# A gated product transposed by VectorE and two queues instead of TensorE, and two top-k rounds moved later

## The chip, the cores and the metric

The kernel runs on one core of a Trainium2 chip. The metric is the device time of one launch in microseconds (us); lower is better. The core has five engines with a queue each: TensorE (PE, with its weight loads shown as PEld), VectorE (DVE), ScalarE (ACT), GpSimd (POOL) and SyncE (SP, which only issues transfers).

## The reference

One decoder block over 512 tokens of width 1024, in float32. Two token mixers run beside each other; their gated sum is projected and added to the input, and a squared-ReLU MLP follows.

```
h = rmsnorm(x); proj = h @ w_in         # u, v_g, q, k, v, q_idx, k_idx, w_idx, gates
# branch a: spatial gating, in 4 chunks c of 128 tokens and 4 groups g of 128 channels
v_g = layernorm(gelu(v_g))
s   = einsum('gts,bcsgd->bctgd', tril(w_s), v_g) + b_s
y_a = gelu(u) * s                        # the "gated product", 512 x 512
# branch b: attention over the 128 keys with the highest index score (top-k)
score = sum_h w_idx * relu(q_idx @ k_idx^T), causal;  sel = top_k(score, 128)
y_b = softmax(rope(q) @ rope(k)[sel]^T / 8) @ v[sel]
merged = sig(g0) * (y_a @ w_out_a) + sig(g1) * (y_b @ w_out_b)
x = x + merged @ w_o
x = x + relu(rmsnorm(x) @ w_ff_in)^2 @ w_ff_out
return rmsnorm(x)
```

## The kernel before

Every float32 product is made of three TensorE passes on split operands: each operand is written as a high part in a matmul format and a low part that holds the remainder (`split`, line 50: ACT copies the high part, DVE or POOL subtracts to get the low part). Weights come in tiles of 128 x 1024 numbers in a fixed sequence: `w_load` issues the transfer (on ACT's queue for the first 24, on SP's after that), `w_conv` splits it (the subtraction of tile 24 and later is DVE's, "wl"), and using tile n calls for the conversion of tiles n+1 and n+2. The buffers are two raw tiles and three of each part.

The program is one list. Products are generators (`gemm`): one step is three matmuls. `fill(n)` lets the next n steps of the queued generators run at that place of the program, so that TensorE has work while VectorE does something else. Evacuations are called one step after the last product (`later`, `tick`). A planner then orders each engine's instructions: it plays the program with modelled costs, takes among the ready instructions the one that stands first in the program, and gives tile slots from the pools as they come free. `keep_in_program_order` pins an instruction behind the one that was written just before it for its engine. Transposed products and evacuations use two pools of four PSUM tiles each, "ps" (gates, keys, queries, the products oa) and "pa" (spatial products, transposes, scores).

The stretch around the change, in the order of the program:

- Lines 535 to 542: 16 rounds of top-k on the index scores `sc[1..3]` (384 query rows in three tiles). In a round, MAX8 finds the eight largest of each row and MATCH_REPLACE marks them as taken. Each round is followed by `fill(5)`; the layer norm of v_g is woven into some. Lines 543 and 544 turn the marks into a mask that is added to the attention scores.
- Line 569: the keys' projection (first four heads) starts; its rotation (`rope`, lines 342 to 356) runs on DVE once both halves are there: four products with cosR and sinR (L347, L348), two sums (L349), and the splits (L351, L352). `k_done` then copies the parts by 32 transfers on POOL's queue into the layout of the scores.
- Lines 574 to 580: the spatial products sg, 12 matmuls of 512 columns, read as four runs of 128; DVE makes the gated product in place in `u` (L579): tokens lie on partitions.
- Lines 583 to 590: the queries' projection is queued. The products `y_a @ w_out_a` need the channels on partitions, so TensorE transposes `u` in 16 blocks of 128 x 128 into PSUM (L588, "yt"), four at a time behind each step of the queries; ACT copies the high part yaTh (L589), DVE subtracts for the low part yaTl (L590).
- Lines 594 to 619: gate gb (first tile), then the products oa of branch a (`branch_a`, eight tiles of 12 matmuls) follow, each evacuated by DVE (L611). The heads of the attention begin behind six of the oa tiles.

At the end of the kernel, `ff_last` makes the last output tile in two column halves (L942 adds a half, L1011 sums its squares, L1015 multiplies it by the gain), POOL raises the mean square to the power -1/2 (L1014), and `store` scales and stores the rows.

Of the kernel before, what the change touches and what calls it, by code (L numbers as in the profile page):

```python
# [12 lines left out]
AF = mybir.ActivationFunctionType  # L13
ALU = mybir.AluOpType

P = 128
# [17 lines left out]
def hybrid_block_kernel(ctx: ExitStack, tc: tile.TileContext, A: dict, out: bass.AP):  # L34
# [9 lines left out]
    def bank(name, tag="ps"):  # L44
        return ps.tile([P, 512], F32, tag=tag, bufs=4, name=name)

    def f32(ap):
        return ap.bitcast(F32)
# [10 lines left out]
    def half(tag, bufs, name):  # L59
        pool, dt = (G, F32) if tag == "yb" else (E, FR)  # L60
        return pool.tile([P, 4, S], dt, tag=tag, bufs=bufs, name=name)
# [26 lines left out]
    def fill(n):  # L88
        while n > 0 and todo:
            try:  # L90
                next(todo[0])
                n -= 1
                tick()
            except StopIteration:
                todo.pop(0)
# [436 lines left out]
            yield  # L532

    ln = layer_norm()
    for n in range(TOPK // 8):
        for i in range(NT - 1, 0, -1):
            DVE.max(out=m8[i], in_=sc[i])
        for i in range(NT - 1, 0, -1):
            DVE.match_replace(out=sc[i], in_to_replace=m8[i], in_values=sc[i], imm_value=TAKEN)
        if n >= 4:  # L540
            next(ln, None)
        fill(5)
    for i in range(1, NT):
        DVE.tensor_scalar(sc[i], sc[i], TAKEN, -BIG, op0=ALU.is_gt, op1=ALU.mult)
    while todo:
        fill(8)

# [21 lines left out]
    fill(12)  # L569
    u = dst_uv["u"]  # L570
    vgh, vgl = vghl
    yaT = [half("ybt", 2, f"yaT{c}") for c in "hl"]
    for g in range(4):
        b = bank(f"sg{g}", "pa")
        c = slice(g * P, (g + 1) * P)
        PE.matmul(b, wsh[:, g], vgl[:, :, c], start=True, stop=False)
        PE.matmul(b, wsl[:, g], vgh[:, :, c], start=False, stop=False)
        PE.matmul(b, wsh[:, g], vgh[:, :, c], start=False, stop=True)
        DVE.scalar_tensor_tensor(u[:, :, c], b.rearrange("p (c d) -> p c d", d=P), bs[:, g:g + 1],  # L579
                                 u[:, :, c], op0=ALU.add, op1=ALU.mult)  # L580
    fill(4)
    todo.append(rope_tiles(W_Q0, "q0", q_done))
    fill(11)
    for g in range(4):
        fill(1)
        b = bank(f"yt{g}", "pa")
        for c in range(NT):
            tc.keep_in_program_order(PE.transpose(b[:, c * P:(c + 1) * P], u[:, c, g * P:(g + 1) * P], ident))  # L588
        ACT.activation(yaT[0][:, g], b, AF.Copy)  # L589
        DVE.tensor_tensor(yaT[1][:, g], b, f32(yaT[0][:, g]), op=ALU.subtract)  # L590
    while todo:
        fill(8)

# [13 lines left out]
    def branch_a(m):  # L607
        b = bank(f"oa{m}")

        def evac():  # L610
            DVE.tensor_tensor(mA[m], b, mA[m], op=ALU.mult)  # L611
        yield from gemm(b, W_OA[m], [yaT[0][:, k] for k in range(4)], [yaT[1][:, k] for k in range(4)], evac)


    todo.append(gate_b(0))
# [350 lines left out]
    def ff_last(fs):  # L966
        def term(dst, w, j, q, k, cols, first, last):
            wh, wl = w[q]
            t = slice(j * P, (j + 1) * P)
            fh, fl = fs[2 * q + k]  # L970
            PE.matmul(dst, fl[:, t], wh[:, k, cols], start=first, stop=False)
            PE.matmul(dst, fh[:, t], wl[:, k, cols], start=False, stop=False)
            PE.matmul(dst, fh[:, t], wh[:, k, cols], start=False, stop=last)
            tick()

        for c in range(2):
            b = [bank(f"f2_{c}_{j}", "pa") for j in range(NT)]
            ws_ = W_F2[c]
            w = {}

            def part(j, q):
                if q not in w:
                    w[q] = w_get(ws_[q], S)
                for k in range(2):
                    term(b[j], w, j, q, k, slice(0, S), q == 0 and k == 0, q == 1 and k == 1)
                if j == 0:
                    w_ahead(ws_[q])
                if q == 1:
                    a = acc[j][:, c * S:(c + 1) * S]
                    add_to(a, b[j], j)  # L990
                    finish(j, c)

            for j, q in [(j, q) for j in range(NT) for q in range(2)] if c else \
                    [(j, q) for q in range(2) for j in range(NT)]:
                if (c, j) != (1, NT - 1):
                    part(j, q)


        j = NT - 1
        bh = [b[j][:, :SH], bank("f2_last", "ps")[:, :SH]]  # L1000
        s = fss[:, j]
        gated[j] = tmp(f"fo{j}")
        store(j - 1)
        for n in range(2):
            cols = slice(n * SH, (n + 1) * SH)
            for q in range(2):
                for k in range(2):
                    term(bh[n], w, j, q, k, cols, q == 0 and k == 0, q == 1 and k == 1)
            a = acc[j][:, S + n * SH:S + (n + 1) * SH]
            add_to(a, bh[n], j)  # L1010
            DVE.tensor_tensor_reduce(out=jk2[:, cols], in0=a, in1=a, op0=ALU.mult, op1=ALU.add, scale=1.0 / D,  # L1011
                                     scalar=s[:, 2 - n:3 - n], accum_out=s[:, 1 + 2 * n:2 + 2 * n])
            if n == 1:
                POOL.tensor_tensor(s[:, 3:4], s[:, 3:4], mhalf[:, :1], op=ALU.pow)  # L1014
            DVE.tensor_tensor(gated[j][:, cols], a, gF[1][:, cols], op=ALU.mult)  # L1015

    fss = G.tile([P, NT, 4], F32, name="fss")
    gated = {}
# [28 lines left out]
    def store(j):  # L1047
        s = fss[:, j, 3:4]
        a, b = acc[j][:, :S], gated[j]
        if j == NT - 2:  # L1050
            ACT.activation(a, a, AF.Copy, scale=s)
        else:
            DVE.tensor_scalar(a, a, s, None, op0=ALU.mult)
        ACT.activation(b, b, AF.Copy, scale=s)
        nc.sync.dma_start(out[j * P:(j + 1) * P, :S], a)
        (nc.scalar if j == NT - 1 else nc.sync).dma_start(out[j * P:(j + 1) * P, S:], b)

    raw_load(0)
    raw_load(1)
# [35 lines left out]
def _col_tiles(w, cols):  # L1095

    k = w.shape[0] // P
    t = w[:, cols].reshape(k, P, -1, P)
    return np.ascontiguousarray(t.transpose(2, 1, 0, 3)).reshape(-1, P, k * P)
# [11 lines left out]
def _layout(x, norm1_g, w_in, w_s, b_s, sgu_ln_g, sgu_ln_b, w_out_a, w_out_b, w_o,  # L1111
            norm2_g, w_ff_in, w_ff_out, norm_f_g):
    c = np.ascontiguousarray
    x = np.asarray(x)[0]
    w = np.asarray(w_in)[0]
    cos, sin = _tables()
    k = KD
    a = {}
    a["xT"] = c(x.T.reshape(k, P, S).transpose(1, 0, 2))
    a["xn"] = c(x.reshape(NT, P, D).transpose(1, 0, 2))  # L1120
    g1 = np.asarray(norm1_g)[0].reshape(k, P).T
    a["x0"] = c(np.concatenate([g1, np.zeros_like(g1), a["xT"][:, 0]], axis=1))

    rows = np.arange(D).reshape(4, KD, 32).transpose(1, 0, 2).reshape(-1)
    a["xr"] = c(x.T[rows].reshape(k, P, S).transpose(1, 0, 2))
    a["g2"] = c(np.asarray(norm2_g)[0][rows].reshape(k, P).T)
    a["gf"] = c(np.asarray(norm_f_g).reshape(1, D))
    a["wa"] = c(np.concatenate([w[:, 2048:2560], w[:, 3072:3144]], axis=1).reshape(k, P, 584).transpose(1, 0, 2))
    cols = _rope_cols(2560) + _rope_cols(1536) + _rope_cols(1024) + list(range(3144, 5192))
    a["wt"] = _col_tiles(w, cols)  # L1130
    a["wuv"] = c(w[:, :1024].reshape(4, 2, P, 2, S).transpose(3, 0, 2, 1, 4)).reshape(8, P, 2 * S)
    a["ws"] = c(np.asarray(w_s)[0].transpose(2, 0, 1))
    a["bs"] = c(np.asarray(b_s)[0].T)
    a["lng"] = c(np.asarray(sgu_ln_g).reshape(1, S))
    a["lnb"] = c(np.asarray(sgu_ln_b).reshape(1, S))

    def pairs(t):
        n, p, f = t.shape
        return c(t.reshape(n // 2, 2, p, f).transpose(0, 2, 1, 3)).reshape(n // 2, p, 2 * f)

    a["woa"] = pairs(_col_tiles(np.asarray(w_out_a)[0], slice(None)))
    a["wob"] = pairs(_col_tiles(np.asarray(w_out_b)[0], slice(None)))
    a["wo"] = _col_tiles(np.asarray(w_o)[0], rows)
    a["f1"] = _col_tiles(np.asarray(w_ff_in)[0][rows], slice(None))
    f2 = np.asarray(w_ff_out)[0].reshape(16, 2, P, 2, S)
    a["f2"] = c(f2[14:].transpose(0, 3, 2, 1, 4)).reshape(4, P, 2 * S)
    a["f2p"] = c(f2[:14].transpose(0, 2, 1, 3, 4)).reshape(14, P, 4 * S)
    a["cs"] = c(np.stack([np.tile(cos.T, (4, 1)), np.tile(sin.T, (4, 1))], axis=1))
    a["csn"] = c(np.stack([cos, sin]).reshape(2, NT, P, 32).transpose(2, 0, 1, 3))
    return a  # L1150
# [17 lines left out]
```

## Time and profile before

| | us |
|---|---|
| time, median of 3 runs (692.12 to 692.24) | 692.13 |
| the profiled execution's own time | 692.15 |
| its span | 690.4 |
| PE busy | 682.8 (99%) |
| DVE busy | 549.3 (80%) |
| ACT busy | 341.3 (49%) |
| POOL busy | 136.4 (20%) |

Times in the rows are microseconds from the start of the span. A row of the order of time has the start, the duration, the engine, the line, the operation, what is written and read, its shape, how many instructions were merged in the row (x4), and in brackets for how long the engine had been idle before and what ended that. Matmuls are pipelined: a matmul of 512 columns is shown with 0.39, and the next one starts about 0.23 after it. The granted TensorE clock was full (0.999) over the span.

### The profile page before, as it was taken

What the parts mean: (1) busy time and instruction counts of PE and PEld (TensorE: products, weight loads), DVE (VectorE), ACT (ScalarE), POOL (GpSimd) and SP (SyncE); (2) the same over time, 40 slices, a digit from 0 to 9 for tenths busy, and PEclk for the clock granted to TensorE, in tenths of its full rate; (3) what the DMA queues carried; (4) which work ended last, traced back from release to release, by engine and by line L of the source; (5) the groups of instructions that cost most, each with busy time, mean ns of one, the idle gap of its engine ahead of it and who ended that gap; (6) DMA issues with size and microseconds to landing.
All of it is one profiled execution on the core that took longest, in us unless ns stands there. A gap on an engine that the chain in (4) does not pass through costs nothing.

```text
span 690.4 us, 8970 instructions
## 1 busy us (share of the span) xinstructions
PE 682.8 (99%) x3207; PEld 574.2 (83%) x3207; DVE 549.3 (80%) x1013; ACT 341.3 (49%) x593; POOL 136.4 (20%) x178
## 2 busy tenths in 40 slices
PE   9999999999999999999999999999999999999996
PEld 8998888888888888888888888888888888888885
DVE  5584999999768978786658756978788797878996
ACT  6634644432345636573336765366562635546143
POOL 0044347862730850000027000000000000000001
PEclk9999999999999999999999999999999999999999
DMA  8736122332841651324358332232333224134023
GB/s 323 273 99 196 63 95 86 98 94 66 246 143 62 168 169 62 108 76 149 125 195 229 96 122 91 88 127 61 130 114 122 77 67 163 61 122 123 0 62 122
DMA packets 26844, 84.12 MB, mean 122 GB/s; under 512 B 5168, under 2 KB 6832, under 8 KB 24752
## 3 DMA queue, kind: packets, MB, share of 16 engines
q1 hardware_dynamic: 16944, 48.38, 22.0%
q10 hardware_dynamic: 5760, 26.78, 11.3%
q0 software_dynamic: 4096, 8.40, 4.7%
q8 instruction: 25, 0.41, 0.3%
q14 instruction: 19, 0.16, 0.1%
HBM read 71.48 MB, written 2.10 MB: 107 GB/s over the span
## 4 chain that ended last, share of the span: by engine, by line
PE 98%; DVE 0%; issue 0%; ACT 0%; POOLq 0%; POOL 0%
PE f L159 8%; PE f L160 8%; PE f L158 8%; PE pp L927 6%; PE pp L928 6%; PE pp L926 6%; PE va L298 4%; PE gb L160 2%; PE gb L158 2%; PE gb L159 2%; PE wo L160 2%; PE ga L159 2%; PE ga L158 2%; PE wo L159 2%; PE wo L158 2%; PE ga L160 2%
## 5 line engine op out<-in xcount | busy, mean ns | idle before, releaser
L51 ACT ACTIVATE wh<-wr 128x1024 fp32r<-128x1024 f32 x88 | 92.8, 1056 | 77.8 <-issue 16.6
L52 DVE TENSOR_TENSOR wl<-wr,wh 128x1024 fp32r<-128x1024 f32 x67 | 81.4, 1218 | 28.6 <-ACT wh L51 28.5
L158 PE MATMUL f<-h2h,wl 128*128 128x512 f32 x256 | 99.6, 389 | 0.0
L159 PE MATMUL f<-h2l,wh 128*128 128x512 f32 x256 | 99.6, 389 | 0.0
L160 PE MATMUL f<-h2h,wh 128*128 128x512 f32 x256 | 99.6, 389 | 0.0
L51 ACT ACTIVATE u<-w2r 128x512 fp32r<-128x512 f32 x98 | 59.0, 625 | 75.7 <-DVE w2r L857 28.1
L927 PE MATMUL pp<-u,fp 128*128 128x512 f32 x196 | 76.2, 389 | 0.0
L928 PE MATMUL pp<-u,fp 128*128 128x512 f32 x196 | 76.2, 389 | 0.0
L52 DVE TENSOR_TENSOR u<-w2r,u 128x512 fp32r<-128x512 f32 x98 | 64.1, 684 | 12.3 <-ACT u L51 12.3
L926 PE MATMUL pp<-u,fp 128*128 128x512 f32 x196 | 72.0, 389 | 0.0
L938 DVE TENSOR_TENSOR P<-pp,P 128x512 f32<-128x512 f32 x84 | 54.4, 683 | 16.6 <-PE pp L928 16.6
L52 POOL TENSOR_TENSOR wl<-wr,wh 128x1024 fp32r<-128x1024 f32 x21 | 52.6, 2504 | 47.9 <-ACT wh L51 46.1
L1023 POOL TENSOR_TENSOR fss<-fss,mhalf 128x1 f32<-128x1 f32 x3 | 1.7, 558 | 302.3 <-DVE fss L1022 302.3
L158 PEld LDWEIGHTS f<-h2h,wl 128*128 128x128 f32 x256 | 48.0, 188 | 10.1
L159 PEld LDWEIGHTS f<-h2l,wh 128*128 128x128 f32 x256 | 48.0, 188 | 10.0
L160 PEld LDWEIGHTS f<-h2h,wh 128*128 128x128 f32 x256 | 48.0, 188 | 9.9
L885 ACT ACTIVATE fr<-f 128x512 f32<-128x512 f32 x32 | 19.1, 598 | 58.2 <-PE f L160 58.0
L926 PEld LDWEIGHTS pp<-u,fp 128*128 128x128 f32 x196 | 36.8, 188 | 7.7
L927 PEld LDWEIGHTS pp<-u,fp 128*128 128x128 f32 x196 | 36.8, 188 | 7.6
L928 PEld LDWEIGHTS pp<-u,fp 128*128 128x128 f32 x196 | 36.8, 188 | 7.6
L369 POOL DMA_DIRECT2D kq<-k_T x64 | 32.1, 508 | 45.7 <-ACT k_T L51 26.4
L822 POOL DMA_DIRECT2D acc<-x1B x32 | 17.0, 537 | 105.9 <-ACT h2h L790 99.9
(268 smaller groups left out, 1615.1 us busy)
## 6 DMA issues: line engine op xcount, KB each, us to landing
wr<-in_f SPq DMA_DIRECT2D x36, 512.0 KB, 3.6
w2r<-in_f2p ACTq DMA_DIRECT2D x14, 1024.0 KB, 4.9
wr<-in_wt SPq DMA_DIRECT2D x14, 512.0 KB, 4.3
wr<-in_wt ACTq DMA_DIRECT2D x14, 512.0 KB, 3.5
wr<-in_wuv ACTq DMA_DIRECT2D x8, 512.0 KB, 4.1
kq<-k_T POOLq DMA_DIRECT2D x64, 64.0 KB, 3.4
wr<-in_wo SPq DMA_DIRECT2D x8, 512.0 KB, 3.5
xn<-in_xn SPq DMA_DIRECT2D x2, 1024.0 KB, 7.9
```

What stands on the lines that cost most here:

```text
L51: ACT.activation(hi, src, AF.Copy)
L52: (eng or DVE).tensor_tensor(lo, src, f32(hi), op=ALU.subtract)
L158: PE.matmul(dst, wl[:, k], bh, start=(k == 0), stop=False)
L159: PE.matmul(dst, wh[:, k], bl, start=False, stop=False)
L160: PE.matmul(dst, wh[:, k], bh, start=False, stop=(k == K - 1))
L298: PE.matmul(acc[j][n][:, :CUT[n].stop - CUT[n].start], a[:, j * P:(j + 1) * P], b[:, CUT[n]], start=(k == 0 and q == 0), stop=(k == KD - 1 ...
L369: eng.dma_start(f32(dst[32 * c:32 * c + 32, :]), f32(T[o][32 * hh:32 * hh + 32, :]))
L885: ACT.activation(r, b, AF.Relu)
L926: PE.matmul(b[j], fl, u[:, 0], start=(q == 0), stop=False)
L927: PE.matmul(b[j], fh, u[:, 1], start=False, stop=False)
L928: PE.matmul(b[j], fh, u[:, 0], start=False, stop=(q == 1))
L938: DVE.tensor_tensor(sums[name, j], b[j], sums[name, j], op=ALU.add)
```

## The change

Part one: the gated product is transposed without TensorE. VectorE transposes `u` in blocks of 32 x 32, four instructions of 128 x 512 (one for each chunk of tokens), into a tile `uB`; then 16 transfers of 64 KB (32 partitions of 512 numbers), eight on SP's queue and eight on POOL's, put each group of 32 partitions in its place in `yaR`. Channels then lie on partitions in another order than before, which the host's layout of `w_out_a` follows, and tokens lie in runs of 32 in another order, which the products oa (they read four runs of 128) and their evacuation (it reads PSUM in runs of 32) undo. ACT and DVE split `yaR` from SBUF. Part two: two of the 16 top-k rounds, and the masks, stand behind these splits, pinned in place. Part three: at the end, the gain is multiplied in behind both sums of squares, and the last tile's second half is scaled in two pieces by ACT and DVE and stored in two transfers.

```diff
-    for n in range(TOPK // 8):
+
+    def topk_round(pin=lambda ins: ins):
         for i in range(NT - 1, 0, -1):
-            DVE.max(out=m8[i], in_=sc[i])
+            pin(DVE.max(out=m8[i], in_=sc[i]))
         for i in range(NT - 1, 0, -1):
             DVE.match_replace(out=sc[i], in_to_replace=m8[i], in_values=sc[i], imm_value=TAKEN)
+    LATE = 2
+    for n in range(TOPK // 8 - LATE):
+        topk_round()
         if n >= 4:
             next(ln, None)
         fill(5)
-    for i in range(1, NT):
-        DVE.tensor_scalar(sc[i], sc[i], TAKEN, -BIG, op0=ALU.is_gt, op1=ALU.mult)
...
-    yaT = [half("ybt", 2, f"yaT{c}") for c in "hl"]
     for g in range(4):
...
+    uB = f32(half("ybt", 2, "uB"))
+    for c in range(NT):
+        tc.keep_in_program_order(DVE.transpose(
+            uB.rearrange("p q (b c e) -> p (q b) c e", c=NT, e=32)[:, :, c],
+            u[:, c].rearrange("p (b e) -> p b e", e=32)))
+    yaR = half("yb", 2, "yaR")
+    for a in range(4):
+        for q in range(4):
+            (nc.sync if q % 2 else nc.gpsimd).dma_start(yaR[32 * q:32 * q + 32, a], uB[32 * a:32 * a + 32, q])
     fill(4)
     todo.append(rope_tiles(W_Q0, "q0", q_done))
-    fill(11)
-    for g in range(4):
-        fill(1)
-        b = bank(f"yt{g}", "pa")
-        for c in range(NT):
-            tc.keep_in_program_order(PE.transpose(b[:, c * P:(c + 1) * P], u[:, c, g * P:(g + 1) * P], ident))
-        ACT.activation(yaT[0][:, g], b, AF.Copy)
-        DVE.tensor_tensor(yaT[1][:, g], b, f32(yaT[0][:, g]), op=ALU.subtract)
+    yaT = [half("ybt", 2, f"yaT{c}") for c in "hl"]
+    for a in range(4):
+        split(yaT[0][:, a], yaT[1][:, a], yaR[:, a])
+        fill(2)
+    for n in range(LATE):
+        topk_round(tc.keep_in_program_order)
+        fill(3)
+    for i in range(1, NT):
+        DVE.tensor_scalar(sc[i], sc[i], TAKEN, -BIG, op0=ALU.is_gt, op1=ALU.mult)
+    yaT = [[t.rearrange("p a (g t) -> p g a t", g=4)[:, g] for g in range(4)] for t in yaT]
...
         def evac():
-            DVE.tensor_tensor(mA[m], b, mA[m], op=ALU.mult)
-        yield from gemm(b, W_OA[m], [yaT[0][:, k] for k in range(4)], [yaT[1][:, k] for k in range(4)], evac)
+            z = mA[m].rearrange("p (c a e) -> p c a e", c=NT, a=4)
+            DVE.tensor_tensor(z, b.rearrange("p (a c e) -> p c a e", a=4, c=NT), z, op=ALU.mult)
+        yield from gemm(b.rearrange("p (a t) -> p a t", a=4), W_OA[m], yaT[0], yaT[1], evac)
...
-            DVE.tensor_tensor(gated[j][:, cols], a, gF[1][:, cols], op=ALU.mult)
+        for n in range(2):
+            cols = slice(n * SH, (n + 1) * SH)
+            tc.keep_in_program_order(DVE.tensor_tensor(
+                gated[j][:, cols], acc[j][:, S + n * SH:S + (n + 1) * SH], gF[1][:, cols], op=ALU.mult))
...
+        if j == NT - 1:
+            ACT.activation(b[:, :SH], b[:, :SH], AF.Copy, scale=s)
+            DVE.tensor_scalar(b[:, SH:], b[:, SH:], s, None, op0=ALU.mult)
+            nc.sync.dma_start(out[rows, :S], a)
+            nc.scalar.dma_start(out[rows, S:S + SH], b[:, :SH])
+            nc.sync.dma_start(out[rows, S + SH:], b[:, SH:])
+            return
...
+    ya_rows = np.arange(S).reshape(4, 4, 32).transpose(1, 0, 2).reshape(-1)
+    a["woa"] = pairs(_col_tiles(np.asarray(w_out_a)[0][ya_rows], slice(None)))
```

## Rows read from the trace of the kernel before

**Rows 1.** The profile page: chain that ended last, share of the span by engine.

```profile
PE 98%; DVE 0%; issue 0%; ACT 0%; POOLq 0%; POOL 0%
```

**Rows 2.** Waits of PE in the whole span: total us, times, longest.

```profile
PE va L302 <- DVE wah L278: 1.1, 1, 1.1
```

**Rows 3.** Order of time of PE, 153 to 194 us: start, duration, instruction.

```profile
153.08 0.39 PE L576 MATMUL sg<-vgl,ws 128*128 128x512 f32 x1
...
155.80 0.39 PE L158 MATMUL k<-hTh,wl 128*128 128x512 f32 x1
...
166.68 0.60 PE L588 MATMUL yt<-ident,u 128*128 128x128 f32 x4
...
171.22 0.40 PE L158 MATMUL gb<-hTh,wl 128*128 128x512 f32 x1
...
176.70 0.39 PE L158 MATMUL oa<-yaTh,wl 128*128 128x512 f32 x1
...
179.42 0.39 PE L158 MATMUL oa<-yaTh,wl 128*128 128x512 f32 x1
...
193.02 0.28 PE L640 MATMUL at<-kq,kq 128*128 128x256 f32 x1
```

**Rows 4.** Order of time of DVE, 154 to 178 us.

```profile
154.46 1.47 DVE L537 MAX8 m<-sc 128x8 f32<-128x512 f32 x3
...
160.39 0.88 DVE L544 TENSOR_SCALAR sc<-sc 128x384 f32<-128x384 f32 x3
161.19 0.68 DVE L347 TENSOR_TENSOR k_a<-k,cosR 128x512 f32<-128x512 f32 x1
161.79 2.71 DVE L579 SCALAR_TENSOR_TENSOR u<-sg,lnt,u 128x512 f32<-128x512 f32 x4
...
168.69 1.21 DVE L52 TENSOR_TENSOR wl<-wr,wh 128x1024 fp32r<-128x1024 f32 x1
...
172.16 2.47 DVE L590 TENSOR_TENSOR yaTl<-yt,yaTh 128x512 fp32r<-128x512 f32 x4
...
175.16 0.67 DVE L347 TENSOR_TENSOR q_a<-q,cosR 128x512 f32<-128x512 f32 x1
...
176.35 0.68 DVE L348 TENSOR_TENSOR q_b<-q,sinR 128x512 f32<-128x512 f32 x1
176.96 1.21 DVE L52 TENSOR_TENSOR wl<-wr,wh 128x1024 fp32r<-128x1024 f32 x1
```

**Rows 5.** Order of time of all engines and queues, 683 to 687 us.

```profile
683.62 0.28 PE L973 MATMUL f_last<-wh,fp 128*128 128x256 f32 x1
...
683.85 0.42 DVE L1015 TENSOR_TENSOR fo<-acc,gF 128x256 f32<-128x256 f32 x1
684.18 0.48 DVE L942 SCALAR_TENSOR_TENSOR acc<-f_last,sq,acc 128x256 f32<-128x256 f32 x1
...
685.27 0.66 POOL L1014 TENSOR_TENSOR fss<-fss,mhalf 128x1 f32<-128x1 f32 x1 [1.64 <-DVE fss L1011]
...
685.97 0.48 DVE L1053 TENSOR_SCALAR acc<-acc,fss 128x512 f32<-128x512 f32 x1 [0.44 <-POOL fss L1014]
...
686.72 0.35 ACTq L1056 DMA_DIRECT2D out<-fo  x1
```

**Rows 6.** Tile x1B: ns min/median/max, first and last start, and its transfers' landing.

```profile
L792 DVE STREAM_TRANSPOSE x1B<-xr x8: 711/712/714, 317.8 to 355.4; 128x512 f32<-128x512 f32 x8
...
DMA to landing us min/median/max: 1.9/4.4/7.4
```

**Rows 7.** Tile kq, 160 to 200 us; then the order of time of POOL.

```profile
L369 POOL DMA_DIRECT2D kq<-k_T x32: 498/498/709, 167.5 to 186.9; - x32
...
DMA to landing us min/median/max: 1.8/3.8/6.1
167.54 1.33 POOL L369 DMA_DIRECT2D kq<-k_T  x2 [13.39 <-DVE k_T L351]
...
187.40 2.74 POOL L369 DMA_DIRECT2D kq<-q_T  x5
```

More of the change, by code (lines that the diff above doesn't have):

```diff
@@ L1053, in store @@
             DVE.tensor_scalar(a, a, s, None, op0=ALU.mult)
+        rows = slice(j * P, (j + 1) * P)
+        if j == NT - 1:
[5 more added lines that the diff above has]
+            return
         ACT.activation(b, b, AF.Copy, scale=s)
-        nc.sync.dma_start(out[j * P:(j + 1) * P, :S], a)
-        (nc.scalar if j == NT - 1 else nc.sync).dma_start(out[j * P:(j + 1) * P, S:], b)
+        nc.sync.dma_start(out[rows, :S], a)
+        nc.sync.dma_start(out[rows, S:], b)
     raw_load(0)
@@ L1139, in pairs @@
         return c(t.reshape(n // 2, 2, p, f).transpose(0, 2, 1, 3)).reshape(n // 2, p, 2 * f)
-    a["woa"] = pairs(_col_tiles(np.asarray(w_out_a)[0], slice(None)))
+    ya_rows = np.arange(S).reshape(4, 4, 32).transpose(1, 0, 2).reshape(-1)
+    a["woa"] = pairs(_col_tiles(np.asarray(w_out_a)[0][ya_rows], slice(None)))
     a["wob"] = pairs(_col_tiles(np.asarray(w_out_b)[0], slice(None)))
```

## The prediction

> **What bounds the kernel now.** I read the chain that ended last first: it is TensorE for 98% of the span [rows 1]. The waits of PE come next: in the whole span PE waited once, 1.1 us, at the start [rows 2]. So a microsecond taken off PE's stream is a microsecond of time, if nothing that PE needs is then late. What is nearly late is seen in the order of time of the stretch from 153 to 182 us. PE runs through it without a gap: the spatial products sg, the second half of the keys, the queries, the first gate gb, the products oa [rows 3]. DVE runs there without a gap too, with the same inputs in hand some microseconds late: the last two top-k rounds end at 160.39, and the rotation's products of the queries end at 177.03, although PE had finished the queries at 171.2 [rows 4]. So PE is the bound, and DVE is the engine whose lateness could become the next one. At the tail, the chain is DVE, POOL, ACT and the last store [rows 5].
>
> I sum against the profiled execution: 692.15 us, of which 690.4 are the span and 1.75 lie around it. It is 0.02 above the median, 692.13. 0.2% is 1.38 us, about what a measurement of this kernel can tell from no change.
>
> **PE: the 16 transposes go.** From the first transpose, 166.68, to gb, 171.22, are 4.54 us [rows 3]. In them stand 12 products of the queries, and 12 such products take 2.72 (oa from 176.70 to 179.42). The rest, 1.82 us, is the transposes: that is the gain, -1.82. PE's needs move forward by it: gb to 169.40, the first oa to 174.88, the second oa to 177.60, the third to 180.32, the first attention scores to 191.20.
>
> **PE: the products oa read four runs of 128 columns.** The sg products read the same four runs (vgl, vgh), and 12 of them take 2.72 us as well (153.08 to 155.80) [rows 3]: the same pace, cost 0. The evacuation of oa reads PSUM in runs of 32. No row shows that; the nearest is the block transpose, which writes in such runs: 712 ns for 512 elements [rows 6]. Even at twice that it hides under the 2.72 us of the next oa.
>
> **DVE: what is added, and in which order.** Four block transposes are added. The operation is in the kernel in the same form: 712 ns [rows 6]. On DVE the next instruction starts 0.08 ahead of the end of the one before (160.39 + 0.88 against 161.19 [rows 4]), so four take 4 x 0.63 = 2.53 us. The four subtractions of yaTl stay, now from SBUF: 2.40 before (172.16 to 174.56), taken as 2.40; the same shape with another source, so 0.2 either way. The two moved rounds are 160.39 - 154.46 = 5.93 us, and the masks 0.80 [rows 4]. Today DVE does from 161.19 to 176.96, in 15.77 us, all of this stretch: gated product, keys' rotation, two weight subtractions, yaTl, the queries' four products. Without the two rounds it starts this at 154.46 (the sg products end at about 156, and it needs the last of them only two microseconds after its start; the keys end at about 158.7, 12 products of 2.72 us behind 155.80 and a little for the last to drain [rows 3]). The late rounds are pinned behind the splits, so the queries' rotation, which the code gives later, comes behind them and the masks. Its four products end at 154.46 + 15.77 + 2.53 + 5.93 + 0.80 = 179.49: everything is only 2.53 us later than today, because the rounds were not dropped but moved.
>
> **The wait that this makes.** The pool of PSUM tiles for keys, queries, gb and oa has four. gb and the first oa take the keys' two; the second oa needs one of the queries'. Today the third product of the rotation ends at 175.83 and the fourth at 177.03, and the second oa starts at 179.42: 3.6 and 2.4 us to spare [rows 3, 4]. After the change they end at 178.36 and 179.56, and it would start at 177.60. One tile is free after the third product, so PE waits 0.76, with the semaphore 0.8; for the other one it would be 2.0. I take 0.8, since the planner gives the tile that is free first. Bounds: 0, if the planner puts the queries' rotation ahead of a late round, and 4.2 (below). Behind this wait PE's whole queue stands, so it is paid in full. Next late is the weight subtraction of the third oa: today it starts at 176.96, right behind the fourth product, so it ends at about 180.7, against 180.32 + 0.8: in time.
>
> **The copies.** They start when the fourth transpose ends: 154.46 + 0.60 + 2.63 (one product of the rotation, then the gated product, 2.71 less 0.08 [rows 4]) + 2.53 = 160.2; for POOL's start I allow 0.3 more. Eight on POOL at 0.50 [rows 7] put its last at 164.0. SP's eight at the 0.35 of a hardware queue [rows 5] are done sooner. Landing: SBUF to SBUF copies of this size take 1.8 to 6.1 us, median 3.8 [rows 7], and 1.9 to 7.4, median 4.4, for the residual's [rows 6]. With 3.8 the last is there at 167.8. The low half of the split needs all 16, since its tile lies where uB lay. DVE is meanwhile at what stands today between 161.19 and yaTl at 172.16, 10.97 us: after the gated product the rest of the keys' rotation, two weight subtractions (1.21 less 0.08 each) and the first product of the queries. It comes to the splits at 154.46 + 10.97 + 2.53 = 167.96. So the landing is just hidden: 0. If that cover is gone, each microsecond of waiting is one of the stall above. Behind the splits that wait stand, on DVE, the pinned rounds; on ACT, one weight copy that is not needed before 174.88; on SP, the next weight load, which waits for the first weight subtraction (168.69 today) anyway. Behind POOL's eight stand the 32 copies of the keys: they start today at 167.54 [rows 7], then at about 164.5, so the queries' copies, today from 187.40 for scores at 193.02 [rows 3, 7], come three microseconds earlier for scores that come one earlier: 0.
>
> **Tail.** Today DVE multiplies by the gain (0.42, from 683.85) before it adds the last half, at 684.18, although PE's last product ended at 683.90 [rows 5]. With the multiplications behind the second sum, DVE starts at 683.95: -0.23 on the way to the power on POOL (today 685.27). The two multiplications then end at 685.66, before the power does, at 685.70. The final scaling starts at 685.74 instead of 685.97 and is split: DVE's first half takes 0.48 as today, so SP stores it at about 686.25, and SP's second store follows an issue (0.35) later, at 686.6, where ACT's stands today at 686.72. All 512 KB must still go out. I take -0.25, between -0.1 and -0.5.
>
> **Sum.** 692.15 - 1.82 + 0.8 - 0.25 = 690.9 us.
>
> **Rivals.**
> (B) No stall: the planner finds room for the queries' rotation ahead of a late round. 692.15 - 1.82 - 0.25 = 690.1. For it: today the planner does put instructions with ready inputs ahead of earlier ones. Against it: the rounds wait for nothing, and are pinned one behind the other.
> (C) The splits stand on DVE ahead of the two weight subtractions. DVE is then at them at 165.1 (167.96 less the 2.86 of the two subtractions and the queries' product) and sits until the copies land, at 165.8 to 167.8: 0.7 to 2.7 us more on the stall, 1.5 to 3.5, so 691.6 to 693.6, in the middle 692.6. The first weight subtraction would then come late for gb too (169.40), but that wait lies within the same delay. For it: DVE does wait for such copies today when the planner took them as landed.
> (D) Slower: POOL's copies land late. Place: the split's wait in front of the pinned rounds. Price: with the longest landing of the rows, 7.4 [rows 6], the last is there at 171.4, DVE sits 3.4, PE waits 4.2: 692.15 - 1.82 + 4.2 - 0.25 = 694.3. It decides from a stall of 3.45 on, which is a landing of 6.6 us. For it: 16 copies at once on two queues. Against it: longest landings belong to stretches with 32 copies and weight loads at once.
> The Trainium skill speaks for D. Its page SBUF — State Buffer says ("Who interferes with whom") that the descriptors of a DMA issued from POOL are written over a port that DVE holds during its two-port modes, and ("A bandwidth-pool intuition that's wrong") that a 620 ns one took 3100 ns beside a DVE copy; by that figure eight would take 24.8 us, and the time would be near 710 (an estimate). The trace does not agree: POOL's issues take 498 ns, at most 709, while DVE is busy [rows 7].
>
> **How the numbers follow.** Forecast 0.42 (690.3 to 691.4, the stall between 0.2 and 1.3); B 0.24; C 0.22; D 0.12. The bound for faster, 690.75, cuts the forecast: 0.17 of it below, 0.25 above. Faster 0.24 + 0.17 = 0.41; slower, from 693.5, D and 0.02 of C: 0.14; the same 0.45. Range 689.9 to 693.3: from B with the largest tail gain to C's upper part.
>
> **What would show it.** Right: no yt on PE; 12 products of the queries in a row; a wait of PE on a DVE product of the queries (L348 or L347 of before) at the second oa, of about 0.8; DVE without a gap from 154 to 178; the masks at 176 to 177; the last addition on DVE within 0.1 of PE's last product. Wrong: a gap on DVE that a copy of uB ends (C, D), a PE wait for a weight subtraction at gb, no PE wait at all (B), the queries' rotation ahead of the second late round, or a changed pace of the oa products. If PE then waits elsewhere, in the attention stage say, the argument that all behind oa moves along is wrong.

## The result, and the profile after

| kernel | median us (runs, range) | ratio to before (95% interval) | PE's wait in the stretch, by its profile |
|---|---|---|---|
| after, first runs | 695.85 (4, 694.77 to 696.70) | 1.0052 (1.0039 to 1.0064) | 3.2 at the second oa |
| after, run again | 695.12 (4, 694.94 to 695.38) | 1.0046 (1.0029 to 1.0063) | 2.9 at the second oa |

The kernel became slower by about half a per cent. Forecast were 690.9 us and a range up to 693.3: wrong in sign, and outside the range. The profiled execution of after took 694.77, the fastest of the eight, and 2.62 more than that of before. Where these 2.62 are, by the views of after:

The chain that ended last, by engine (it was PE 98% before [rows 1]):

```profile
PE 93%; DVE 3%; DMA 1%; POOL 1%; issue 0%; SPq 0%; POOLq 0%; ACT 0%; DVEq 0%
```

The waits of PE in the whole span (total us, times, longest); the second one was there before [rows 2]:

```profile
PE oa L158 <- DVE q_a L347: 3.2, 1, 3.2
PE va L302 <- DVE wah L278: 1.1, 1, 1.1
```

PE in order of time, from the first gate on:

```profile
169.07 0.39 PE L158 MATMUL gb<-hTh,wl 128*128 128x512 f32 x1
...
174.51 0.39 PE L158 MATMUL oa<-yaTh,wl 128*128 128x512 f32 x1
...
177.00 0.39 PE L160 MATMUL oa<-yaTh,wh 128*128 128x512 f32 x1
180.57 0.50 PE L158 MATMUL oa<-yaTh,wl 128*128 128x512 f32 x1 [3.18 <-DVE q_a L347]
180.90 0.39 PE L159 MATMUL oa<-yaTl,wh 128*128 128x512 f32 x1
...
181.85 0.63 PE L160 MATMUL oa<-yaTh,wh 128*128 128x512 f32 x1
182.27 0.63 PE L158 MATMUL oa<-yaTh,wl 128*128 128x512 f32 x1
182.70 0.63 PE L159 MATMUL oa<-yaTl,wh 128*128 128x512 f32 x1
...
185.24 0.39 PE L159 MATMUL oa<-yaTl,wh 128*128 128x512 f32 x1
```

The gate gb starts 2.15 us earlier than before [rows 3]; 0.33 of this was there already at the spatial products (152.75 against 153.08), so the transposes gave the forecast's 1.82. Then the second oa starts 6.06 us after the first instead of 2.72: a stall of 3.34. The first matmuls behind it still come at the old pace; from 181.85 on, 1.3 us after PE went on, they come 0.43 us apart instead of 0.227, until 185.2. The same stretch by windows (the columns are PE, PEld, DVE, ACT and POOL busy, then the granted clock as PEclk, the DMA share and GB/s):

```profile
176.00:180.00 4.00, 1.39 (x7) 0.81 (x5) 4.00 (x14) 0.00 (x0) 4.00 (x8) 1.00 0.44 107
180.00:184.00 4.00, 3.43 (x11) 2.71 (x12) 4.00 (x7) 1.15 (x2) 4.00 (x9) 0.72 0.61 140
184.00:188.00 4.00, 4.00 (x17) 3.26 (x16) 2.44 (x5) 0.84 (x2) 1.28 (x3) 0.85 0.93 249
```

A mean of 0.72 over four us and 0.85 over the next four is 2.24 + 1.20 = 3.44 us at half, the 1.2 GHz level. What it costs is read from the starts: the 13 steps from 180.57 to 185.24 take 4.67 us instead of 13 x 0.227 = 2.95, so 1.72. The sum is -0.33 - 1.82 + 3.34 + 1.72 - 0.17 (tail, below) = +2.74, beside +2.62 measured.

Why the queries' products were late, in DVE's order of time:

```profile
167.06 0.68 DVE L347 TENSOR_TENSOR q_a<-q,cosR 128x512 f32<-128x512 f32 x1
170.09 2.50 DVE L52 TENSOR_TENSOR yaTl<-yaR,yaTh 128x512 fp32r<-128x512 f32 x4 [2.35 <-DMA kq<-k_T]
172.51 1.47 DVE L538 MAX8 m<-sc 128x8 f32<-128x512 f32 x3
...
178.43 0.88 DVE L605 TENSOR_SCALAR sc<-sc 128x384 f32<-128x384 f32 x3
179.24 0.68 DVE L348 TENSOR_TENSOR q_b<-q,sinR 128x512 f32<-128x512 f32 x1
179.84 0.68 DVE L347 TENSOR_TENSOR q_a<-q,cosR 128x512 f32<-128x512 f32 x1
...
181.63 1.21 DVE L52 TENSOR_TENSOR wl<-wr,wh 128x1024 fp32r<-128x1024 f32 x1
```

The order is the forecast's to the instruction, and DVE comes to the splits at 167.7 (forecast 167.96). There it sits for 2.35 us. The transfer named as releaser is one of the keys'; the transfers share semaphores, and ACT, which needs four of the copies for its last high part, names the copies themselves:

```profile
169.43 0.63 ACT L51 ACTIVATE yaTh<-yaR 128x512 fp32r<-128x512 f32 x1 [2.28 <-DMA yaR<-uB]
```

Tile yaR, ns min/median/max of the issues, first and last start, and the landing:

```profile
L594 SPq DMA_DIRECT2D yaR<-uB x8: 507/587/738, 160.0 to 164.7; - x8
L594 POOL DMA_DIRECT2D yaR<-uB x8: 498/498/709, 160.3 to 163.9; - x8
...
DMA to landing us min/median/max: 2.0/2.8/4.6
```

The tail, in order of time of all engines:

```profile
686.49 0.28 PE L990 MATMUL f_last<-wh,fp 128*128 128x256 f32 x1
...
686.81 0.48 DVE L959 SCALAR_TENSOR_TENSOR acc<-f_last,sq,acc 128x256 f32<-128x256 f32 x1
...
687.90 0.66 POOL L1031 TENSOR_TENSOR fss<-fss,mhalf 128x1 f32<-128x1 f32 x1 [1.40 <-DVE fss L1028]
```

From PE's last matmul's start to POOL's power it is 1.41 us (1.65 before [rows 5]); to the end of the span 6.61 (693.1 less 686.49) against 6.78 (690.4 less 683.62): -0.17.

### The profile page after: what moved, and what is told of

It is laid out like the page before. It is cut to its first block, busy times and chain, and to the rows that moved or that the text cites. A ratio compares the mean times of both kernels' runs of the same rounds, so it can differ in the third digit from the quotient of the medians.

```text
span 693.1 us, 8988 instructions
## 1 busy us (share of the span) xinstructions
PE 682.3 (98%) x3191; PEld 572.8 (83%) x3191; DVE 552.5 (80%) x1018; ACT 341.1 (49%) x593; POOL 140.8 (20%) x186
## 4 chain that ended last, share of the span: by engine, by line
PE 93%; DVE 3%; DMA 1%; POOL 1%; issue 0%; SPq 0%; POOLq 0%; ACT 0%; DVEq 0%
PE f L158 8%; PE f L160 8%; PE f L159 8%; PE pp L945 6%; PE pp L943 6%; PE pp L944 6%; PE va L298 3%; PE ga L159 2%; PE ga L158 2%; PE wo L159 2%; PE wo L158 2%; PE wo L160 2%; PE ga L160 2%; PE gb L159 2%; PE gb L160 2%; PE gb L158 2%
```

## The experiments

My theory: DVE is late as a whole, because it sits for the copies with the late rounds queued behind, and the clock adds its 1.72 us to that. Rivals: the copies alone stop PE; only one PSUM tile is short; the rounds hurt by their new place; the half clock has another cause.

| kernel | median us (runs, range) | ratio to before (interval) | PE's wait, us |
|---|---|---|---|
| rounds behind the queries | 689.86 (6, 689.36 to 690.47) | 0.9968 (0.9956 to 0.9980) | none |
| second oa from the other pool | 695.72 (4, 693.26 to 695.89) | 1.0044 (1.0030 to 1.0059) | 3.1, third oa |
| PE kept busy | 693.59 (10, 692.81 to 694.57) | 1.0023 (1.0014 to 1.0032) | 0.2 |
| tail alone | 691.68 (11, 691.31 to 691.96) | 0.9995 (0.9986 to 1.0004) | none |
| round, split, round | 690.80 (11, 690.56 to 691.49) | 0.9982 (0.9973 to 0.9991) | 0.7, second oa |
| copies on three queues | 693.83 (10, 691.46 to 694.39) | 1.0019 (1.0010 to 1.0028) | 1.9, second oa |
| no late rounds | 694.17 (6, 693.55 to 695.00) | 1.0030 (1.0019 to 1.0042) | 3.0, gb |
| late rounds alone | 692.97 (10, 692.57 to 693.24) | 1.0014 (1.0005 to 1.0023) | 0.5, second oa |

### The rounds behind the queries' rotation

```diff
+    while todo:
+        fill(8)
     for n in range(LATE):
         topk_round(tc.keep_in_program_order)
-        fill(3)
...
-    while todo:
-        fill(8)
```

> The kernel after, with the two late rounds and the masks moved once more: behind the rotation of the queries instead of in front of it. DVE still sits until the copies land. Theory (the wait is made by the rounds in front of the queries' products): no wait of PE at the second oa, a full clock throughout, and the transposes' 1.82 us and the tail's 0.17 are kept: 692.1 - 1.8 - 0.2 = 690.1 us (689.8 to 690.5). Rival (the late copies alone are enough to stop PE, at the first or second oa): a wait of 1 us or more on a DVE product or on yaTl, 691.5 us or more. Second rival (what the rounds delay only comes later, in the attention stage): no wait at oa but one of 1 us or more on DVE's first softmax rows, 691.5 or more.

Measured: 689.86, no wait at the oa products, clock 1.00 in every window from 150 to 220. DVE in order of time:

```profile
170.04 2.50 DVE L52 TENSOR_TENSOR yaTl<-yaR,yaTh 128x512 fp32r<-128x512 f32 x4 [2.23 <-DMA wr<-in_woa]
...
174.25 0.69 DVE L348 TENSOR_TENSOR q_b<-q,sinR 128x512 f32<-128x512 f32 x1
...
190.19 1.47 DVE L538 MAX8 m<-sc 128x8 f32<-128x512 f32 x3
```

DVE still sits 2.23 us for the copies, and PE doesn't notice: the queries' last product starts at 174.25 instead of 181.03. The first rival falls. The rounds, moved to 190, still end in front of the first row that needs the masks, and PE doesn't wait there; the second rival falls too. This version beats both kernels: before by 2.3 us, after by 5.3 to 6.0.

### The second oa's tile from the other pool

```diff
-        b = bank(f"oa{m}")
+        b = bank(f"oa{m}", "pa" if m == 1 else "ps")
```

> The kernel after, with the PSUM tile of the second oa alone taken from the other pool, so that it doesn't wait for one of the queries'. Theory (DVE as a whole is late, the tile is only the first thing it owes): PE doesn't wait at the second oa but at the third, for the weight subtraction that DVE ends at about 182.8 and that is needed at about 180.0, so 2.5 to 3 us in place of 3.2, and the time stays within 0.7 us of the kernel after. Rival (only the tile is short): no wait, full clock, 690.1 us.

The waits of PE:

```profile
PE oa L158 <- DVE wl L52: 3.1, 1, 3.1
```

The second oa runs on, and the third waits for the weight subtraction instead. The tile was only the first thing that DVE owed. One of the four runs, at a mean clock of 0.999, took 693.26; the three at 0.993 took 695.6 to 695.9.

### PE kept busy in the wait

```diff
+    def pad():
+        b = bank("pad", "pa")
+        for n in range(14):
+            tc.keep_in_program_order(PE.matmul(b, hTh[0][:, :P], hTh[1], start=True, stop=True))
...
+        if m == 0:
+            todo.append(pad())
```

> The kernel after, with 14 products whose result nobody reads between the first and the second oa, so that PE works where it now waits. They take 14 x 0.227 = 3.2 us, as long as the wait. Theory (the granted clock falls to half because PE idled in the wait): the second oa starts where it starts now, within 0.3 us, no stretch at half clock behind it, and the time is 1.7 us lower than the run of the kernel after with the short half-clock stretch (694.8), 693.1 us (692.7 to 693.5), with all runs close together. Rival (the stretch at half clock has another cause): it stays, and the time is 694.8 to 696.7 as now.

PE in order of time, then the windows:

```profile
177.86 3.33 PE L635 MATMUL pad<-hTh,hTh 128*128 128x512 f32 x14
181.40 0.50 PE L158 MATMUL oa<-yaTh,wl 128*128 128x512 f32 x1 [0.20 <-DVE q_a L347]
```

```profile
176.00:180.00 4.00, 4.00 (x19) 3.30 (x19) 4.00 (x13) 0.56 (x1) 4.00 (x9) 1.00 0.48 118
180.00:184.00 4.00, 3.80 (x17) 2.83 (x16) 4.00 (x7) 0.63 (x1) 4.00 (x9) 1.00 0.51 136
184.00:188.00 4.00, 4.00 (x19) 3.30 (x18) 3.21 (x5) 0.72 (x2) 1.30 (x3) 1.00 0.85 236
```

The second oa starts 6.26 us after the first (175.14), no sooner than in after (6.06, and 5.76 in its second profile), and no stretch is at half. The ten runs have mean clocks of 0.997 to 0.999 and lie 1.5 (695.12) to 2.3 us (695.85) under the medians of after: idling is what brought the half clock. The median is 0.5 above my number and just above my range; the profile starts the oa products 0.6 us later than the first profile of after does. The second profile of after does that too (175.13), so it is a difference between executions, not this edit's.

### The tail alone

The kernel before, with the third part of the change only.

> The kernel before with the change of the tail alone. Theory (from the profile of after, whose stretch from PE's last product to the end is 0.17 us shorter): -0.17 us (-0.1 to -0.3). Rival (nothing of it reaches the end, the last store sets it): within 0.05 us of the kernel before.

-0.47 by medians, with an interval of -0.14% to +0.04%: no change can't be excluded. In its profile it is 6.57 us from the start of the last matmul (683.43) to the end (690.0), against 6.78: -0.21. The size that I expected is the trace's; the times don't decide it.

### One round in front of the splits

```diff
+    fill(9)
+    topk_round(tc.keep_in_program_order)
     yaT = [half("ybt", 2, f"yaT{c}") for c in "hl"]
     for a in range(4):
         split(yaT[0][:, a], yaT[1][:, a], yaR[:, a])
-        fill(2)
-    for n in range(LATE):
-        topk_round(tc.keep_in_program_order)
-        fill(3)
+    topk_round(tc.keep_in_program_order)
+    fill(6)
```

> The kernel after with the first late round, the four subtractions of yaTl and the second late round in this order, behind the second weight subtraction: while the last copies land, DVE does a round instead of sitting. The work in front of the queries' last product stays the same. Theory (the stall is the forecast's 0.8 us plus the 2.35 us that DVE sat for the copies, one for one): DVE comes to the subtractions at about 170.0, when the last copy is there, and doesn't sit; the queries' product L347 that frees the tile ends at about 178.0, the second oa would start at 177.2, so PE waits 0.8 us (0.5 to 1.2); without a fall of the clock the time is 692.1 - 1.8 - 0.2 + 0.8 = 690.9 us (690.5 to 691.4), with one 1.5 to 2.5 us more. Rival (the stall doesn't come from the sitting): it stays at 2.5 us or more, 693 us or more.

The wait of PE, and DVE in order of time:

```profile
PE oa L158 <- DVE q_a L347: 0.7, 1, 0.7
```

```profile
170.58 2.48 DVE L52 TENSOR_TENSOR yaTl<-yaR,yaTh 128x512 fp32r<-128x512 f32 x4
...
177.95 0.68 DVE L347 TENSOR_TENSOR q_a<-q,cosR 128x512 f32<-128x512 f32 x1
```

The row of yaTl has no bracket: DVE came to it only behind the last copy (there at 170.0) and did not sit. The same work in front of the queries' products, without the 2.35 us of sitting, gives the forecast's 0.8 us of stall (0.7) and its time (690.9; 690.80). No run's mean clock was under 0.997.

### The copies on three queues

```diff
-            (nc.sync if q % 2 else nc.gpsimd).dma_start(...)
+            (nc.gpsimd, nc.sync, nc.scalar)[(4 * a + q) % 3].dma_start(...)
```

> The kernel after with the 16 copies in turn on the queues of POOL (6), SP (5) and ACT (5); the planner then also puts the second weight subtraction of DVE between the two late rounds. Theory (the issue of eight copies at 0.59 us on SP sets the last landing): the last copy is issued at about 163 instead of 164.8 and there at about 167.3 instead of 169.4, DVE sits about 1 us, and the wait of PE at the second oa is shorter by 1 us, 2.2 us (the weight subtraction now counts in it). Rival (the transport sets it, beside the keys' copies and the weight loads): the last copy lands later than 168.7, and the stall is 3 us or more.

Tile yaR, as above; then the wait of PE and a window:

```profile
L594 POOL DMA_DIRECT2D yaR<-uB x6: 496/497/709, 160.6 to 163.2; - x6
L594 SPq DMA_DIRECT2D yaR<-uB x5: 507/593/964, 160.3 to 163.7; - x5
L594 ACTq DMA_DIRECT2D yaR<-uB x5: 593/612/859, 160.3 to 163.3; - x5
...
L52 DVE TENSOR_TENSOR yaTl<-yaR,yaTh x4: 684/684/693, 168.2 to 170.0; 128x512 fp32r<-128x512 f32 x4
...
DMA to landing us min/median/max: 1.9/3.3/4.1
```

```profile
PE oa L158 <- DVE q_a L347: 1.9, 1, 1.9
```

```profile
180.00:184.00 4.00, 4.00 (x11) 3.12 (x12) 4.00 (x6) 1.66 (x3) 3.12 (x7) 0.57 0.51 108
```

DVE goes on at 168.2 instead of 170.1 and PE waits 1.3 us less. The last issue starts 1.0 earlier, the release comes 1.9 earlier: the issues explain about half of the lateness, and a shorter landing most of the rest (the last copy takes 3.8 us to land instead of 4.6). Eight of the ten runs, at 0.995 or 0.996, took 693.5 to 694.4; the two at 0.998 took 691.46 and 691.92: the clock's price is about 2 us, as much as the wait itself.

### No late rounds, and the late rounds alone

LATE = 0 in after:

> The kernel after with all 16 rounds and the masks in front of the keys' rotation, as before the change; transposes on DVE, copies and tail as in after. Theory (what counts is the sum of DVE's work ahead of the queries' last product, and the late rounds are in it in after too): everything of DVE's from k_a on comes 6.7 us later and without the rounds, the last copy lands at about 176.1, the first yaTl is done at about 177, so PE waits some 2.7 us in the first oa, and some 0.5 more at the second: 3 us together, a stretch at half clock behind it, 694 to 696.5 us, as the kernel after. Rival (the late place of the rounds does help): slower than the kernel after by 1 us or more.

Right in sum, wrong in place: PE waits 3.0 us already at gb, for the weight subtraction that now starts at 171.5, and then no more. The runs are 0.95 us (695.12 less 694.17) to 1.7 (695.85) under after; this one's profile shows no half clock, and the two of its six runs with a mean of 0.998 took 693.55 and 693.56. So the rounds' late place, as after has it, bought nothing.

```profile
PE gb L158 <- DVE wl L52: 3.0, 1, 3.0
```

The kernel before with the rounds moved behind yaTl, TensorE's transposes kept:

> The kernel before, TensorE's transposes kept, with the two rounds and the masks moved behind the subtractions of yaTl; no block transposes, no copies, the old tail. Theory (the late rounds alone tip nothing, since DVE only does the same work in another order): the queries' products end at about 177, as before, 2.4 us before the second oa needs the tile; no wait of PE, 692.1 us (within 0.3). Rival (rounds in front of the queries' products are harmful in themselves): a wait at the second oa, 693 us or more.

Here my theory missed: 692.97, 0.83 more, with a wait of 0.5 at the second oa, the rival's sign at just about its time. DVE in order of time shows what I had left out:

```profile
159.00 0.69 DVE L348 TENSOR_TENSOR k_b<-k,sinR 128x512 f32<-128x512 f32 x1 [0.94 <-PE k L160]
...
168.23 0.69 DVE L593 TENSOR_TENSOR yaTl<-yt,yaTh 128x512 fp32r<-128x512 f32 x1 [1.40 <-ACT yaTh L592]
169.37 0.69 DVE L593 TENSOR_TENSOR yaTl<-yt,yaTh 128x512 fp32r<-128x512 f32 x1 [0.44 <-ACT yaTh L592]
...
179.59 0.68 DVE L347 TENSOR_TENSOR q_a<-q,cosR 128x512 f32<-128x512 f32 x1
```

With the rounds gone from in front, DVE comes to each step before its input does, and sits 0.94, 1.40 and three times 0.44 us, 3.67 in all. In the kernel before those six us of rounds were what let the inputs collect [rows 4]. The same work in another order is not the same time.

### The kernel after once more

> The kernel after once more, unchanged. Theory (the wait of 3.2 us is in every run, and the runs differ by how long the clock stays at half behind it): the time is 692.1 - 1.8 - 0.2 + 3.2 = 693.3 us in a run whose clock doesn't fall, 694.8 with the 3.4 us at half of the first profile, up to 696.7 with a longer stretch, and the runs' mean clocks order them so. Rival (the runs differ by the length of the wait): the wait in this profile is not 3.2 us, and runs of the same clock differ by more than 1 us.

```profile
PE oa L158 <- DVE q_a L347: 2.9, 1, 2.9
```

```profile
180.00:184.00 4.00, 3.11 (x8) 2.49 (x9) 4.00 (x7) 0.82 (x2) 4.00 (x9) 0.66 0.49 131
184.00:188.00 4.00, 4.00 (x17) 3.21 (x17) 2.70 (x4) 0.75 (x2) 1.61 (x4) 0.92 1.00 240
```

A wait 0.3 shorter, 3.4 us at half, 695.08. The clocks order the runs only roughly: at 0.995 and 0.996 they took 694.8 to 695.4 without an order. The rival's signs came in part: the wait is not 3.2, but runs of the same clock differ by 0.6 us at most. Of after's eight runs none had a clock above 0.996. The two runs at 0.993 took 696.3 and 696.7, and of those two there is no profile. The kernel with the second oa's tile from the other pool has one at 0.993: its clock is 0.78, 0.50 and 0.86 in the three windows of four us from 180, so 1.76 + 4.00 + 1.12 = 6.9 us at half. That after's two longest runs had such a long stretch too is likely by their clocks, not shown.

## Why the prediction was wrong

- **PE: the 16 transposes go** (-1.82): right, 1.82 at gb. **The products oa read four runs** (0): right, the products of the first oa end at their old pace; their evacuation takes 688 ns and hides.
- **DVE: what is added, and in which order**: the order was right. The queries' third product, forecast to end at 178.36, ended at 180.5. The 2.14 us between are the sitting less 0.2.
- **The copies**: this is the step that failed: the landing was put at "just hidden: 0", and DVE sat 2.35 us for it. "SP's eight at the 0.35 of a hardware queue [rows 5] are done sooner": their median was 0.59, they started 0.67 apart, and SP's last was issued at 164.7, 0.8 behind POOL's. "With 3.8 the last is there at 167.8": it landed 4.6 us after its issue, at 169.3, and DVE started 0.8 after that. So the sitting is 0.7 us of later issue, 0.8 of longer landing, and 0.8 between the landing and DVE's start, for which the forecast had no term. The price of 0.35 came from one store of the output, on ACT's queue [rows 5]. A nearer one stood in the trace of the kernel before: 32 copies of 48 KB within SBUF, issued on SP for the index queries, of 32 partitions like these (tile QSi; ns min/median/max, first and last start):

```profile
L369 SPq DMA_DIRECT2D QSi<-qi_T x32: 507/588/1207, 43.8 to 65.5; - x32
```

At that pace, 32 starts from 43.8 to 65.5 and so 0.70 apart, SP's last would have been issued at 160.2 + 7 x 0.70 = 165.1 and, with the forecast's 3.8, been there at 168.9: 0.9 us of sitting instead of 0. And the cover was "just hidden" by 0.16 us, with landings known to spread over four us [rows 6, 7]: a step with so little to spare should not have been put at 0.

- **The wait that this makes**: the place (second oa, on the tile that q_a frees) and the rule "each microsecond of waiting is one of the stall above" were right: 0.8 + 2.35 is 3.15 beside 3.18 by the profile, and with the sitting gone the wait was 0.7. The term was mis-sized at 0.8.
- **A term that was not there**: what PE's clock does after a wait, 1.7 us in both profiles of after and about 2 between like runs. The Trainium skill, in TensorE: Matmul & The Clock Gate ("HAM oscillation — how this bites in real kernels"), says of another kernel that its waits on data bring the half clock back each time. The runs here agree in the main: it came in 19 of the 22 with a wait of 1.9 to 3.2 us at the oa products. With this term rival D, "692.15 - 1.82 + 4.2 - 0.25", would have been near 696.
- **Rival D** named the place, the split's wait in front of the pinned rounds, and the slower side; its cause was wrong: POOL's issues kept their 498 ns, and SP's were the late ones. The Trainium skill's DMA: Bandwidth & Descriptors ("Issuing engine by pattern") calls the hardware queues of SP and ACT generally faster; for these copies the issue took 587 and 612 ns there (medians), 498 on POOL, so it does not hold for the issue. **B** fell by the pinning, as argued; **C** did not occur.
- **Tail** (-0.25): -0.17 in after, -0.21 alone.

## What to carry to other kernels

A queue of always-ready work in front of a step is a buffer: moving it behind a step that waits for transfers exposes that wait, and everything pinned behind it is late by as much. Put such work behind what the bound engine needs next (here 690.80 with one round in front of the wait, and 689.86 with both behind the queries, out of 695). Price a wait of TensorE at more than its length: behind the waits of 1.9 to 3.2 us seen here mostly came a stretch at half clock that cost about 2 us more. And price an issue by the nearest shape on the same queue.

## What the runs showed that was not expected

The half clock does not follow every wait. Waits of 1.9 to 3.2 us at the oa products were followed by it in most runs of the same kernel (eight of ten, three of four, eight of eight by the mean clocks), not in all. The 3.0 us at gb were followed by it in three of six, and one more, at a mean of 0.997, is unclear; waits of 0.5 and 0.7 in none of 21. What decides is open.

The late landing is one late part of SP's last copy. Each copy lands in 16 parts. In the first profile of after, SP's last copy lands so (us of its parts, from the trace's landing events):

```
167.13 167.36 167.48 ... 167.91 167.97 169.32
```

Fifteen were there by 167.97, the sixteenth 1.35 later. In the same microseconds the chip fetched 16 KB of instructions (the DMA queues of after from 166 to 169 us: packets, MB, share):

```profile
q8 instruction: 1, 0.02, 2.1%
```

In the kernel without late rounds the copies are issued 7 us later (last on SP at 172.1), behind that fetch, and their longest landing is 3.4 us instead of 4.6 with its parts evenly spread:

```profile
DMA to landing us min/median/max: 2.0/2.8/3.4
```

Two of the keys' copies on POOL, issued at 164.4 and 164.9, have one part as late in that profile, 1.34 and 1.35 us behind the other fifteen. The next weight load is issued 0.8 us behind SP's last copy there and 0.7 in the kernel without late rounds, so its timing is not what differs. In six profiles (after twice, the rounds behind the queries, the other pool, PE kept busy, and round, split, round) the last part of SP's last copy is 0.7 to 1.5 us behind the one before. With three queues it is only 0.24, although that copy lands beside the fetch too. That the fetch holds a part up is likely, then, not shown: it was not tried by itself.

In after, DVE starts 0.77 us behind the last landing, ACT 0.1. The trace's list of semaphore waits shows part of the reason. In front of its first low part DVE has a row of waits, two semaphores in each. It passes the one on SP's last copy at 169.35, three more at 169.80, 169.90 and 169.99, and starts at 170.09; ACT passes its own at 169.34 and starts at 169.43. In the kernel without late rounds all four steps take 0.10 us each. Why the first took 0.45 in after is open.
